# One transposing transfer per tile, side products one microsecond behind a freed PSUM bank, and weight loads ahead of turns on SP

## The chip, the cores and the metric

The kernel runs on one core of a Trainium2 chip. The metric is the device time of one execution in microseconds. Three runs of the kernel before gave 1275.52 to 1277.26 us, median 1276.15 us.

Engines are named as in the profile: PE does matmuls (PEld its weight loads), DVE element-wise work on vectors, ACT activation functions and copies, POOL the reductions over partitions, SP issues most DMA transfers.

## The reference, cut to what matters

Two layers, each a mixer of three branches (a retention, a gated linear recurrence "hgrn2", a differential attention) and a feed-forward block with a short convolution. There are 256 tokens behind 16 learned ones, so T = 272 columns; the model width is 1024 and everything is in 32-bit floats.

```python
for li in range(DEPTH):
    h = h + mixer(rms_norm(h, norm_mix_g[li]), w_in[li], w_branch[li], w_out[li], ...)
    h = h + conv_ffn(rms_norm(h, norm_ffn_g[li]), w_ffn_in[li], conv_w, conv_b, w_ffn_out[li], valid)
# mixer:
proj = hn @ w_in                      # 14 groups of columns: rq rk rv rg hq hf hi hg dq dk dv and three gates
branches = [retention(...), hgrn2(...), diff_attention(...)]
y = sum(sigmoid(gate_n) * (branch_n @ w_branch[n]))
return y @ w_out
```

Nearly all arithmetic is in the products with weights: `w_in`, three `w_branch`, `w_out`, `w_ffn_in` and `w_ffn_out`, all of which are streamed from memory once.

## The kernel before, in words

**Main products.** Activations lie with features on the partitions and the 272 tokens in the free direction. A weight tile is 128 by 128. To keep 32-bit precision with faster products, weights and activations are each cut into a high and a low part, and a tile takes three matmuls (lines 953 to 955): high by high, high weight by low activation, low weight by high activation. The last product of the second layer (`final`, lines 1593 to 1595) has weights as the moving side. The list `ORDER` names the products of a layer in their order: the columns of `w_in` (`hq`, `hf`, ..., `m2`), the branch products `b0`, `b1`, `b2`, then `wo`, `fi`, `fo`.

**Weights.** `_Weights.next` takes weights in chunks of eight tiles, 512 KB. For each chunk SP starts one transfer into `wraw` (three buffers), ACT copies it into `whi` with rounding (four buffers), DVE subtracts into `wlo` (four buffers). A chunk feeds 24 matmuls. The ACT and DVE instruction of a chunk carry `due`, the place in the plan's time at which the first matmul needs them; the transfer carries none.

**Side products.** The branches' own matmuls (recurrence levels `lev`, `px`, `pm`; outputs `ho` and `ro`; scores `s` and `ds`; attention outputs `do`) run on PE between main products. Their results lie in PSUM banks of two rotating buffers each, `bank` and `acc`. A bank is free again when the last instruction that reads it, on ACT or DVE, is done.

**Turns.** Where data has to be transposed, ACT copies the upper and the lower 16 bits of each 32-bit word into two planes (`apart`), SP starts a transposing transfer for each plane (`turned`), and ACT puts the planes together again. This happens in `to_tokens` (values of all branches, blocks of 128 columns, four to a plane), `flip` (one block to a plane), `da_rest` (three blocks to a plane) and `residual` (four). There are 61 such tiles, so 122 transposing transfers.

**The order of the work.** The program is first recorded as a list of operations, and a planner (`_Plan.order`) then simulates the engines with costs given in the code and emits all instructions in the order in which the simulation started them. On the chip each engine takes its instructions in this order and waits at each one for what it needs; an instruction that waits holds up all behind it on its engine. The names in the planner that matter here:

- `start(op, t)`: the earliest time at which an operation finds all buffers it needs (a buffer of a tag comes free when its last user is done, plus a lag).
- `rank(op, t)`: among operations of an engine that can start at the same time, the lowest rank goes first. A side product is not taken until the data that others gave it has been there for `SAFE` = 1.0 us. An operation whose `due` is less than `URGENT` = 3 ahead of the main product last started goes before everything else.
- `LAG`: time from the end of an operation until another engine may use its result; 2.0 us for SP's transfers.
- in `_Engine.call`: the cost of a transfer on SP is 0.06 us, plus its bytes over 360 GB/s, plus 0.7 us when it transposes. So a plane of four blocks counts 1.49 us, a weight chunk 1.52 us.
- `behind` and `settle` spread the side work of a branch over the main products that run beside it; `*b2` cuts the result of the differential attention into `b2hi` and `b2lo` for the product `b2`.

Of the kernel before, what the change touches and what calls it, by code (L numbers as in the profile page):

```python
# [21 lines left out]
P = 128  # L22
# [17 lines left out]
SLOTS = 13  # L40
# [8 lines left out]
HOLD, PULL = 3.0, 8.0  # L49
SAFE = 1.0  # L50
SURE = 0.3
URGENT = 3


BASE = {"rq": 0, "rk": 4, "rv": 8, "rg": 16, "hq": 24, "hf": 32, "hi": 40, "hg": 48,
# [300 lines left out]
class _Plan:  # L356
# [99 lines left out]
    def order(self):  # L456
# [29 lines left out]
        def start(op, t):  # L486

            want = {}
            for n in op.tiles:
                if n not in held:  # L490
                    want[self.tag[n]] = want.get(self.tag[n], 0) + 1
            for tag, k in want.items():
                if len(free[tag]) < k:
                    return None
                t = max(t, sorted(free[tag])[k - 1])
            return t

        def rank(op, t):
            if op.engine == "pe" and op not in mains:
                if op.fed + SAFE > t:  # L500
                    return math.inf
                return op.key - PULL if beside and op.fed + SURE <= t else op.key + HOLD
            if op.due - reached < URGENT:
                return op.due - 1000.0
            late = 8.0 if op.func in self.SETS and self.SETS[op.func] != tables else 0.0
            return op.key + late
# [4 lines left out]
        while len(out) < todo:  # L511
            best = None
            for e, t0 in engines.items():
                while later[e] and later[e][0][0] <= t0:
                    _, c, op = heapq.heappop(later[e])
                    now[e].append((c, op))
                found = None
                for c, op in now[e]:
                    t = start(op, t0)
                    if t is not None and (found is None or (t, rank(op, t), c) < found[:3]):  # L520
                        found = (t, rank(op, t), c, op)
                if later[e]:
                    t1 = later[e][0][0]
                    if found is None or t1 < found[0]:
                        found = (t1, 0.0, -1, None)
                if found is not None and (best is None or found[0] < best[0]):
                    best = found + (e,)
            if best is None:
                raise RuntimeError("no order: " + str([(e, [o.tiles for _, o in now[e]][:4]) for e in now]))
            t, _, c, op, e = best  # L530
            if op is None:
                engines[e] = t
                continue
            now[e].remove((c, op))
            cost = op.cost
            if op.func in self.SETS and self.SETS[op.func] != tables:
                tables = self.SETS[op.func]
                cost += self.SWITCH
                if tables == "le":
                    out.append(None)  # L540
                    todo += 1
            for n in op.tiles:
                if n not in held:
                    held.add(n)
                    f = free[self.tag[n]]
                    f.remove(min(f))
            if e == "pe":
                beside = op not in mains
                if not beside:
                    reached = op.key  # L550
            if e == "pool" and op.func is not None:
                if op.func != code:
                    code, t = op.func, max(t, engines[e] + self.RELOAD)
                engines["dve"] += self.SHARE * max(0.0, min(engines["dve"], t + cost) - t)
                sums.append((t, t + cost))
            if e == "dve":
                cost += self.SHARE * sum(max(0.0, min(b, t + cost) - max(a, t)) for a, b in sums[-2:])
            engines[e] = t + cost
            self.busy[e] += cost
            done = t + cost  # L560
            for n in op.tiles:
                left[n] -= 1
                if left[n] == 0:
                    free[self.tag[n]].append(done + self.LAG[e] + self.FREE)
            for o in op.after:
                o.need -= 1
                if o.engine != e:
                    o.fed = max(o.fed, done + self.LAG[e])
                o.ready = max(o.ready, done + (self.LAG if o.engine != e else self.SAME)[e])
                if o.need == 0:  # L570
                    push(o)
            for o in op.then:
                o.need -= 1
                o.ready = max(o.ready, done)
                if o.need == 0:
                    push(o)
            if op.run is not None:
                out.append(op)
            else:
                todo -= 1  # L580
# [12 lines left out]
class _Engine:  # L593
# [5 lines left out]
    def __getattr__(self, method):  # L599
        f = getattr(self.engine, method)  # L600

        def call(*args, **kw):
# [20 lines left out]
            if method == "reciprocal":  # L623
                cost += 7 * self.each * n
            elif method == "tensor_tensor_scan":
                cost += self.each * n
            elif method == "transpose":
                cost = 0.11
            elif method == "matmul":
                cost = max(0.218 if args[1].shape[-1] > 32 else 0.07, 4 * n / 2400 + 0.02)  # L630
            elif method == "dma_start":
                cost = self.fixed + self.each * n * outs[0].shape[0] + (0.7 if kw.get("transpose") else 0.0)
            self.plan.add(self.name, lambda: f(*args, **kw), cost, outs, ins, kind)  # L633

        return call
# [2 lines left out]
class _Weights:  # L638
# [13 lines left out]
    def next(self):  # L652
        c, i = divmod(self.used, CHUNK_TILES)
        self.used += 1
        if i == 0:
            due = self.plan.key
            room = [P, ROOM]
            raw = self.plan.tile(self.pool, [P, CHUNK_TILES * P], F32, "wraw", 3, f"wraw{c}")
            hi = self.plan.tile(self.pool, room, F32R, "whi", 4, f"whi{c}")
            lo = self.plan.tile(self.pool, room, F32R, "wlo", 4, f"wlo{c}")  # L660
            self.plan.key = due - LEAD
            pieces = 1 if c > 1 else 2
            for p in range(pieces):
                n = CHUNK_TILES // pieces
                cols = slice(p * n * P, (p + 1) * n * P)
                self.sp.dma_start(raw[:, cols], self.w[c][:, cols])
                order, places = self.places[c]
                mine = [[x[i] for i in order[p * n : (p + 1) * n]] for x in places]
                for first, outer, inner, dims in _boxes(*mine):
                    src = self.part(raw, (p * n + first) * P, inner * P, P, outer, inner)  # L670
                    to_hi, to_lo = (self.part(t, *x, outer, inner) for t, x in zip((hi, lo), dims))
                    self.act.activation(to_hi, src, AF.Copy)
                    self.dve.tensor_tensor(out=to_lo, in0=src, in1=to_hi.bitcast(F32), op=SUB)
                    for op in self.plan.ops[-2:]:
                        op.due = due
            self.plan.key = due
            self.cut = hi, lo
        return tuple(t[:, at[i] : at[i] + P] for t, at in zip(self.cut, self.places[c][1]))
# [16 lines left out]
def _trace(ctx, tc, plan, a, depth, probe):  # L695
# [298 lines left out]
    def planes(name, n):  # L994
        return new(tp, [P, 4 * T], U16, "vsrc", 4, name)[:, : 2 * n].rearrange("p (i x) -> p i x", i=2)

    def to_tokens(src, vt, e):

        apart, turned = planes("apart", 4 * P), planes("turned", 4 * P)
# [2 lines left out]
        for i in range(2):  # L1002
            act.activation(apart[:, i].rearrange("p (c f x) -> p c f x", c=2, f=2),
                           halves(src[:, :, : 2 * P], i).rearrange("p f (c x) -> p c f x", c=2), AF.Copy)
        for i in range(2):
            sync.dma_start(turned[:, i].rearrange("p (b x) -> p b x", x=P), apart[:, i], transpose=True)
        turned = turned.rearrange("p i (c x) -> p i c x", c=2)
        if top is None:
            for i in range(2):
# [10 lines left out]
    def flip(out, x):  # L1020
# [3 lines left out]
        halves = lambda t, i: t.bitcast(U16).rearrange("p (x two) -> p x two", two=2)[:, :, i]  # L1024
        for i in range(2):
            act.activation(apart[:, i], halves(x, i), AF.Copy)
        for i in range(2):
            sync.dma_start(turned[:, i].rearrange("p (b x) -> p b x", x=P), apart[:, i], transpose=True)
        for i in range(2):
            act.activation(halves(out, i), turned[:, i], AF.Copy)  # L1030

# [46 lines left out]
    for li in range(depth):  # L1078
# [365 lines left out]
        def da_rest(b, hd, sb, nm, sm, cf, tiles):  # L1444
# [17 lines left out]
            for i in range(2):  # L1462
                for c, n, at in ((0, 2 * P, P), (T, P, 0)):
                    act.activation(apart[:, i, at : at + n], halves(w[:, c : c + n], i), AF.Copy)
            for i in range(2):
                sync.dma_start(turned[:, i].rearrange("p (b x) -> p b x", x=P), apart[:, i], transpose=True)
            for i in range(2):
                act.activation(halves(a1[:, META : T + P], i), turned[:, i], AF.Copy)

# [73 lines left out]
        def residual():  # L1543
# [5 lines left out]
            for g, (t, c) in enumerate(((0, 0), (0, 1), (1, 0))):  # L1549
                apart, turned = planes("apart", 4 * P), planes("turned", 4 * P)  # L1550
                halves = lambda x, i: x.bitcast(U16).rearrange("p k (x two) -> p k x two", two=2)[:, :, :, i]
                for i in range(2):
                    act.activation(apart[:, i].rearrange("p (k x) -> p k x", k=4), halves(h[:, 4 * c : 4 * c + 4, META + t * P : META + (t + 1) * P], i), AF.Copy)
                for i in range(2):
                    sync.dma_start(turned[:, i].rearrange("p (b x) -> p b x", x=P), apart[:, i], transpose=True)
                for i in range(2):
                    act.activation(halves(st["old"][:, g : g + 1], i), turned[:, i].unsqueeze(1), AF.Copy)
                plan.key += 20.0
# [250 lines left out]
```

## Time and profile before

| what | value |
|---|---|
| median of three runs | 1276.15 us |
| lowest and highest | 1275.52, 1277.26 us |
| the profiled execution, its own time | 1276.58 us |
| its span, from the first to the last instruction | 1274.8 us |
| busy time of PE, PEld | 1261.6 and 1240.7 us |
| busy time of DVE, ACT, POOL | 964.8, 899.2, 115.5 us |
| granted clock of PE, mean | 0.999 |
| weight transfers on SP | 402 of 512 KB, 4 of 256 KB |
| transposing transfers on SP | 122 |
| DMA traffic | 230.49 MB, mean 181 GB/s |

How to read the rows: a row of the timeline has the start in us from the span's first instruction, the duration, the engine, the line, the operation, out<-in by the names in the code, and in brackets the idle time of that engine just before, with what ended it. Line 633 is the helper that records every operation, so rows of it are told apart by names. Matmuls overlap in the pipeline and their ends are modelled: a matmul with 272 columns shows some 0.28 us, but the next one starts 0.12 us after it. A short stop of PE is therefore best read from the distance of two starts, and PE's idle time shows less than the stop.

### The profile page before, as it was taken

The numbers are of one execution on the slowest core, as the hardware profiler recorded it, in microseconds if no ns is written. First come the engines' busy times: TensorE is split into PE (matmuls) and PEld (weight loads), VectorE is DVE, ScalarE is ACT, GpSimd is POOL, SyncE is SP. The second block draws the span as 40 slices with busy tenths as digits, with TensorE's granted clock in tenths as the row PEclk, the third lists the DMA queues.
The fourth block names the chain that finished last, engine by engine and source line by source line (L and its number), as shares of the span: only waits on it lengthen the run. The fifth ranks groups of instructions, "written<-read, shape, count | busy, mean of one in ns | idle before, by whom it ended". The sixth has DMA issues, their size and how long they took to land.

```text
span 1274.8 us, 28782 instructions
## 1 busy us (share of the span) xinstructions
PE 1261.6 (99%) x11612; PEld 1240.7 (97%) x11612; DVE 964.8 (76%) x1677; ACT 899.2 (71%) x1700; POOL 115.5 (9%) x89
## 2 busy tenths in 40 slices
PE   9999999999999999999999999999999999999998
PEld 9999999999999999999999999999999999999986
DVE  6797587899775789886576875878897868898854
ACT  6766687788797576665456567887788975787643
POOL 2000031101111000000010000411012210000000
PEclk9999999999999999999999999999999999999999
DMA  7655557556647546556555546475565566576663
GB/s 269 196 168 155 165 152 216 170 152 190 197 142 207 183 151 198 180 170 193 172 180 180 168 145 190 151 228 174 154 190 176 166 202 203 167 213 205 206 196 110
DMA packets 109205, 230.49 MB, mean 181 GB/s; under 512 B 55312, under 2 KB 55440, under 8 KB 109072
## 3 DMA queue, kind: packets, MB, share of 16 engines
q1 hardware_dynamic: 108784, 228.13, 58.0%
q8 instruction: 91, 1.49, 0.5%
q10 hardware_dynamic: 288, 0.52, 0.1%
q14 instruction: 42, 0.34, 0.1%
HBM read 216.16 MB, written 1.05 MB: 170 GB/s over the span
## 4 chain that ended last, share of the span: by engine, by line
PE 84%; issue 5%; DVE 3%; DMA 3%; ACT 3%; POOL 2%; SPq 0%; ACTq 0%; POOLq 0%; DVEq 0%
PE main L953 24%; PE main L955 24%; PE main L954 24%; DMA wraw<-in_w 3%; POOL hr L633 2%; PE fo L1593 2%; PE fo L1594 2%; PE fo L1595 2%; PE lev L1178 1%; DVE wlo L633 1%; PE fi L955 1%; PE fi L954 1%; PE fi L953 1%; ACT whi L633 1%; PE ds L1422 1%
## 5 line engine op out<-in xcount | busy, mean ns | idle before, releaser
L953 PE MATMUL main<-xh,whi 128*128 128x272 f32 (+1 forms) x2240 | 642.6, 287 | 0.7 <-ACT whi L633 0.7
L633 DVE TENSOR_TENSOR wlo<-wraw,whi 128x1024 fp32r<-128x1024 f32 (+1 forms) x411 | 498.4, 1217 | 188.6 <-ACT whi L633 183.1
L955 PE MATMUL main<-xh,wlo 128*128 128x272 f32 (+1 forms) x2240 | 636.9, 284 | 1.2 <-DVE wlo L633 1.0
L954 PE MATMUL main<-xl,whi 128*128 128x272 f32 (+1 forms) x2240 | 636.1, 284 | 1.0 <-issue 1.0
L633 ACT ACTIVATE whi<-wraw 128x1024 fp32r<-128x1024 f32 (+1 forms) x411 | 426.1, 1041 | 195.2 <-PE main L954 78.5
L955 PEld LDWEIGHTS main<-xh,wlo 128*128 128x128 f32 x2240 | 421.6, 188 | 3.5 <-DVE wlo L633 2.2
L953 PEld LDWEIGHTS main<-xh,whi 128*128 128x128 f32 x2240 | 421.7, 188 | 2.2 <-ACT whi L633 1.2
L954 PEld LDWEIGHTS main<-xl,whi 128*128 128x128 f32 x2240 | 421.7, 188 | 0.2
L633 POOL PARTITION_ALL_REDUCE hr<-hsq x36 | 76.9, 2155 | 426.6 <-ACT hsq L633 388.9
L633 DVE SCALAR_TENSOR_TENSOR two_b<-main,small,two_b 128x256 f32<-128x256 f32 (+2 forms) x128 | 54.6, 487 | 28.3 <-ACT two_b L633 28.2
L633 ACT ACTIVATE two_b<-main,small 128x272 f32<-128x272 f32 (+1 forms) x64 | 33.1, 566 | 28.1 <-PE main L955 28.1
L953 PE MATMUL main<-ghi,whi 128*128 128x272 f32 x176 | 50.8, 289 | 0.0
L954 PE MATMUL main<-glo,whi 128*128 128x272 f32 x176 | 50.6, 287 | 0.0
L955 PE MATMUL main<-ghi,wlo 128*128 128x272 f32 x176 | 50.3, 286 | 0.0
L955 PE MATMUL main<-b1hi,wlo 128*128 128x272 f32 (+1 forms) x128 | 36.6, 286 | 1.2 <-DVE wlo L633 1.2
L953 PE MATMUL main<-b0hi,whi 128*128 128x272 f32 (+1 forms) x128 | 37.3, 291 | 0.2 <-DVE y L633 0.2
L953 PE MATMUL main<-b1hi,whi 128*128 128x272 f32 (+1 forms) x128 | 37.1, 290 | 0.0
L953 PE MATMUL main<-yhi,whi 128*128 128x272 f32 (+1 forms) x128 | 36.4, 284 | 0.0
L955 PE MATMUL main<-yhi,wlo 128*128 128x272 f32 (+1 forms) x128 | 36.3, 284 | 0.0
L954 PE MATMUL main<-b0lo,whi 128*128 128x272 f32 (+1 forms) x128 | 36.3, 284 | 0.0
L954 PE MATMUL main<-b1lo,whi 128*128 128x272 f32 (+1 forms) x128 | 36.3, 284 | 0.0
L954 PE MATMUL main<-ylo,whi 128*128 128x272 f32 (+1 forms) x128 | 36.3, 284 | 0.0
(283 smaller groups left out, 2169.2 us busy)
## 6 DMA issues: line engine op xcount, KB each, us to landing
wraw<-in_w SPq DMA_DIRECT2D x402, 512.0 KB, 3.8
turned<-apart SPq DMA_TRANSPOSE x86, 2.7
h<-in_h SPq DMA_DIRECT2D x4, 272.0 KB, 5.6
dec<-in_dec SPq DMA_DIRECT2D x2, 544.0 KB, 6.1
wraw<-in_w SPq DMA_DIRECT2D x4, 256.0 KB, 5.2
const<-in_const SPq DMA_DIRECT2D x1, 937.0 KB, 5.4
turned<-turned SPq DMA_TRANSPOSE x36, 2.4
gain<-in_gl SPq DMA_DIRECT2D x1, 512.0 KB, 5.0
```

Source lines behind the costliest of these rows:

```text
L633: self.plan.add(self.name, lambda: f(*args, **kw), cost, outs, ins, kind)
L953: nc.tensor.matmul(o, wh, hi, start=first, stop=False)
L954: nc.tensor.matmul(o, wh, lo, start=False, stop=False)
L955: nc.tensor.matmul(o, wl, hi, start=False, stop=last)
L1178: nc.tensor.matmul(o, keys, x, start=True, stop=True)
L1422: nc.tensor.matmul(ss[m][:, at : at + nk], q[half, hd, q0 : q0 + P], k[half, hd, :nk], start=True, stop=True)
L1593: nc.tensor.matmul(o, gh, wh, start=first, stop=False)
L1594: nc.tensor.matmul(o, gl, wh, start=False, stop=False)
L1595: nc.tensor.matmul(o, gh, wl, start=False, stop=end)
```

## The change

The planner's rules change in three places, and the two transfers of a tile's planes become one.

```diff
-URGENT = 3
+URGENT = {"act": 4.5, "dve": 3.0, "sp": 12.0}
+TURN = "turn"
+STILL = 0.5
...
             for tag, k in want.items():
                 if len(free[tag]) < k:
                     return None
-                t = max(t, sorted(free[tag])[k - 1])
+                late = SAFE if op.engine == "pe" and op not in mains else 0.0
+                t = max(t, sorted(free[tag])[k - 1] + late)
             return t
...
-            if op.due - reached < URGENT:
+            if op.due - reached < URGENT.get(op.engine, 0.0):
                 return op.due - 1000.0
...
-                o.ready = max(o.ready, done + (self.LAG if o.engine != e else self.SAME)[e])
+                o.ready = max(o.ready, done + (self.LAG if o.engine != e else self.SAME)[e] + STILL * (o.func == TURN))
...
             elif method == "dma_start":
-                cost = self.fixed + self.each * n * outs[0].shape[0] + (0.7 if kw.get("transpose") else 0.0)
+                cost, kind = (1.3, TURN) if kw.get("transpose") else ( self.fixed + self.each * n * outs[0].shape[0], None)
...
                 self.sp.dma_start(raw[:, cols], self.w[c][:, cols])
+                fetch = self.plan.ops[-1]
...
                     for op in self.plan.ops[-2:]:
                         op.due = due
+                    fetch.due = due if c > SLOTS else math.inf
...
+    def turn(out, x):
+
+        sync.dma_start(out.rearrange("p i (b x) -> p (i b) x", x=P), x.rearrange("p i x -> p (i x)"), transpose=True)
+
...
-        for i in range(2):
-            sync.dma_start(turned[:, i].rearrange("p (b x) -> p b x", x=P), apart[:, i], transpose=True)
+        turn(turned, apart)
```

The last edit stands in `to_tokens`, `flip`, `da_rest` and `residual` alike. In words:

- **Banks.** A side product on PE, if it takes a new buffer, is planned no earlier than 1.0 us after that buffer came free. Main products keep the old rule.
- **Turns.** A tile's two planes go in one transfer, which the plan counts at 1.3 us whatever its size. `o.func == TURN` is asked of the operation that is to be made ready, so the 0.5 us of `STILL` lie between the ACT copies into the planes and the start of the transfer.
- **Weights.** From the 15th chunk on, the transfer of a chunk has a `due` too, and SP takes it before anything else that could start at the same time when its first matmul is less than 12 us of plan ahead. For ACT's copy into `whi` this distance grows from 3 to 4.5 us; for DVE it stays at 3. PE and POOL have no operations with a `due`.

More of the change, by code (lines that the diff above doesn't have):

```diff
@@ L1026, in flip @@
             act.activation(apart[:, i], halves(x, i), AF.Copy)
-        for i in range(2):
-            sync.dma_start(turned[:, i].rearrange("p (b x) -> p b x", x=P), apart[:, i], transpose=True)
+        turn(turned, apart)
         for i in range(2):
@@ L1464, in da_rest @@
                     act.activation(apart[:, i, at : at + n], halves(w[:, c : c + n], i), AF.Copy)
-            for i in range(2):
-                sync.dma_start(turned[:, i].rearrange("p (b x) -> p b x", x=P), apart[:, i], transpose=True)
+            turn(turned, apart)
             for i in range(2):
@@ L1553, in residual @@
                     act.activation(apart[:, i].rearrange("p (k x) -> p k x", k=4), halves(h[:, 4 * c : 4 * c + 4, META + t * P : META + (t + 1) * P], i), AF.Copy)
-                for i in range(2):
-                    sync.dma_start(turned[:, i].rearrange("p (b x) -> p b x", x=P), apart[:, i], transpose=True)
+                turn(turned, apart)
                 for i in range(2):
```

## The prediction

> **What bounds the kernel now.** I read the page first, then PE's busy time by stretches, then who PE waited for.
>
> ```profile
> span 1274.8 us, 28782 instructions
> PE 1261.6 (99%) x11612; PEld 1240.7 (97%) x11612; DVE 964.8 (76%) x1677; ACT 899.2 (71%) x1700; POOL 115.5 (9%) x89
> ```
> ```profile
> 0.00:23.00 23.00, 21.11 (x140) 19.82 (x141) 13.47 (x18) 15.15 (x24) 5.58 (x9) 1.00 0.79 255
> ...
> 200.00:400.00 200.00, 198.13 (x1596) 195.06 (x1595) 160.24 (x333) 165.44 (x393) 30.76 (x19) 1.00 0.63 180
> ...
> 900.00:1040.00 140.00, 137.54 (x1150) 134.49 (x1150) 111.19 (x247) 115.75 (x288) 23.70 (x14) 1.00 0.59 177
> ```
> ```profile
> PE main L955 <- DVE wlo L633: 2.2, 4, 0.8
> PE ro L1062 <- DVE ho L633: 1.1, 2, 0.8
> PE main L954 <- issue: 1.0, 1, 1.0
> ...
> PE main L953 <- ACT whi L633: 0.7, 2, 0.4
> PE do L633 <- DVE tw L633: 0.4, 1, 0.4
> ```
>
> PE sets the end: it is busy for 1261.6 of 1274.8 us at full clock (the 1.00 of each stretch), so no amount of faster side work counts unless PE stops for it. The stops lie where the branches run: 1.9 us of idle time in the first layer (200 to 400), 2.5 us in the second (900 to 1040). The list of waits names them: late weights, and `ro` products that wait for DVE's `ho`. The change adds and removes no matmul; it can only gain these stops, a few us out of 1276, and it can lose without such a limit, since the planner deals out the whole order anew. The start (first weights) and the 1.0 us that the profile puts down to nothing are out of its reach.
>
> **Part 1, the banks.** The regular distance of two main matmuls and the stops at side products:
>
> ```profile
> 30.14 0.29 PE L955 MATMUL main<-xh,wlo 128*128 128x272 f32 x1
> 30.26 0.28 PE L953 MATMUL main<-xh,whi 128*128 128x272 f32 x1
> ```
> ```profile
> 233.23 0.28 PE L633 MATMUL ro<-wts,rvt 128*128 128x144 f32 x1
> 233.83 0.39 PE L1062 MATMUL ro<-kt,rvt 128*128 128x272 f32 x1 [0.32 <-ACT tw L633]
> ```
> ```profile
> 242.97 0.36 PE L1062 MATMUL ro<-kt,rvt 128*128 128x272 f32 x1 [0.84 <-DVE ho L633]
> ```
> ```profile
> 242.38 0.79 DVE L633 TENSOR_TENSOR ho<-ro,hr 128x272 f32<-128x272 f32 x2 [1.07 <-ACT hr L633]
> ```
> ```profile
> 260.14 0.36 PE L1062 MATMUL ro<-kt,rvt 128*128 128x272 f32 x1 [0.25 <-DVE ho L633]
> ```
> ```profile
> 326.68 0.29 PE L955 MATMUL main<-b0hi,wlo 128*128 128x272 f32 x1
> 327.00 0.49 PE L633 MATMUL do<-tw,vs 128*128 128x128 f32 x2
> ```
>
> Two starts are 0.12 us apart (30.14 to 30.26). At 233.83 they are 0.60 apart: a stop of 0.48, of which the idle time shows 0.32, so the pipeline hides 0.16. With this 0.16 the stop at 242.97 is 1.00 and the one at 260.14 is 0.41. At 327.00 the distance is 0.32, a stop of 0.20. These four wait for the last reader of a bank: the two `ho` at 242.38 read the two `ro` banks of the head before, and `tw` reads the bank of `ret_tail`. Together 0.48 + 1.00 + 0.41 + 0.20 = 2.09 us.
>
> The edit puts such a product 1.0 us later in PE's order; main products fill the time. It removes no instruction. As the longest stop is just 1.00, it covers all four if the rest of the order stays as it is; I take 1.9 of the 2.09, since the last one is covered without any margin. Bounds: nothing (the readers come later by as much as the product), and 2.09. What it costs is delay of the branch, up to 1 us for each bank taken; that is free while the main products that need the branch are further away. That cover is thinnest before `b2` of the second layer:
>
> ```profile
> 1037.95 1.24 DVE L633 TENSOR_TENSOR b2lo<-da,b2hi 128x1032 fp32r<-128x1032 f32 x1 [0.35 <-ACT b2hi L633]
> ```
> ```profile
> 1039.88 0.28 PE L953 MATMUL main<-b2hi,whi 128*128 128x258 f32 x1
> ```
>
> The second half of `b2`'s input is done at 1039.19. `b2` starts at 1039.88 with four weight tiles for each of two outputs, 24 matmuls of 0.12, from the first half; the second half is needed at 1042.8. The slack is 3.6 us.
>
> **Part 2, one transfer for two planes.**
>
> ```profile
> L633 SPq DMA_TRANSPOSE turned<-apart x86: 1178/1234/2645, 120.1 to 1154.1; - x86
> ...
> L633 SPq DMA_TRANSPOSE turned<-turned x36: 1100/1176/1914, 131.8 to 1019.0; - x36
> ```
> ```profile
> turned<-apart SPq DMA_TRANSPOSE x86, 2.7
> ...
> turned<-turned SPq DMA_TRANSPOSE x36, 2.4
> ```
>
> A transfer of three or four blocks holds SP for 1.234 us, one of a single block for 1.176: three more blocks cost 0.06 us of issue and 0.3 us until landing. A joint transfer of eight blocks is not in the trace. Bounds: issue between 1.2 (as today's one) and 2.5 (as today's two); landing between 2.7 (as today's one) and 1.2 + 2.7 = 3.9 us (as today's second). By the small difference between one and four blocks I take the lower ends, 1.3 us of issue and 3.0 until landing. So 61 tiles give SP back 61 × 1.2 = 73 us in all, and a turn is complete about 0.9 us sooner. The joint transfer must wait for both copies of ACT, where the first plane used to go after its own copy; SP's second issue came 1.2 us after the first anyway, so this costs nothing while the copies are less than that apart. Behind a waiting turn on SP stand weight transfers; with one turn in place of two there is one such wait less per tile. None of this is on PE's path by itself, so I price it at nothing; it pays through part 3. The planned 1.3 us, with 0.5 ahead and the lag of 2.0 behind, leaves 0.3 us for landing beyond my 3.0.
>
> [...]
>
> **Part 3, weights ahead of turns.**
>
> ```profile
> 1011.12 3.54 SPq L633 DMA_DIRECT2D wraw<-in_w  x2
> 1014.81 1.19 SPq L633 DMA_TRANSPOSE turned<-apart  x1
> 1016.67 3.40 SPq L633 DMA_TRANSPOSE turned<-turned  x2
> 1020.12 1.25 SPq L633 DMA_TRANSPOSE turned<-apart  x1
> 1021.47 7.63 SPq L633 DMA_DIRECT2D wraw<-in_w  x4
> ```
> ```profile
> 1018.24 0.50 ACT L633 ACTIVATE hr<-hr,eps 128x242 f32<-128x242 f32 x1 [1.59 <-POOL hr L633]
> ...
> 1026.43 1.06 ACT L633 ACTIVATE whi<-wraw 128x1024 fp32r<-128x1024 f32 x1 [1.48 <-DMA wraw<-in_w]
> 1028.31 1.06 ACT L633 ACTIVATE whi<-wraw 128x1024 fp32r<-128x1024 f32 x1 [0.82 <-DMA wraw<-in_w]
> ```
> ```profile
> 1026.99 0.28 PE L955 MATMUL main<-xh,wlo 128*128 128x258 f32 x1
> 1027.54 0.39 PE L953 MATMUL main<-xh,whi 128*128 128x258 f32 x1 [0.27 <-ACT whi L633]
> 1027.77 0.28 PE L954 MATMUL main<-xl,whi 128*128 128x258 f32 x1
> 1028.80 0.39 PE L955 MATMUL main<-xh,wlo 128*128 128x258 f32 x1 [0.76 <-DVE wlo L633]
> ```
> ```profile
> 988.41 0.39 PE L955 MATMUL main<-b1hi,wlo 128*128 128x258 f32 x1 [0.76 <-DVE wlo L633]
> ```
> ```profile
> 379.66 0.39 PE L955 MATMUL main<-b1hi,wlo 128*128 128x272 f32 x1 [0.43 <-DVE wlo L633]
> ```
>
> Here the whole mechanism is in sight. ACT stands still for POOL until 1018.24; the second turn of the flip on SP waits behind that; from about 1014.7 (end of 3.54 us from 1011.12) to 1021.47 SP starts no weight. PE eats a chunk in 24 × 0.12 = 2.9 us, so more than two chunks are missing. When SP comes free they go out in a row; the first is copied at 1026.43, and PE stops at 1027.54 (0.55 between starts, a stop of 0.43) and at 1028.80 (1.03, a stop of 0.91). That is 1.34 us, and the edit aims at just this: a weight due within 12 us goes before a turn, the turn starts 0.5 us behind ACT's copies, and it is one issue instead of two. I take all 1.34. At 988.41 the idle time is the same 0.76, so the stop is again 0.91; no SP row is at fault there but the order on ACT and DVE. An `act` distance of 4.5 instead of 3 moves the copy 1.5 us up if the planner saw it as late; half of it, 0.45, I count as gained. At 379.66 (0.43 idle, 0.59 with the 0.16) DVE is late and its distance is unchanged: nothing. Part 3 gains 1.34 + 0.45 = 1.8, with bounds from 2.84 (all four) to nothing.
>
> What is moved back: a turn that lets a weight pass lands later. Two transfers in a row are copied at 1026.43 and 1028.31, so each weight in front costs some 1.9 us. On ACT, evacuations and exponentials stand behind an earlier `whi`, 1.06 us each; PE would notice only if a main bank came free late, and the list of waits has no such row now.
>
> **The sum.** A new order brings new stops by chance; data that comes late (0.4 behind `tw` in the list, more such in other places) is in no edit's reach. I put 0.3 us for them, between nothing and the 2.8 of late weights that this order has. So −1.9 − 1.8 + 0.3 = −3.4 us. The profiled execution took 1276.58 us, 1.78 more than its span; it becomes 1273.2. It lies 0.43 above the median of the three runs, so the median becomes 1272.75.
>
> **The rivals.**
>
> *New stops for old ones.* Stops of 0.4 to 1.0 us are errors of the planner's costs, which the edits do not mend except at the banks; late weights turn up elsewhere, because ACT still waits for POOL and SP still takes its order. For it: three of the late weights have three different causes (SP, ACT, DVE). Against it: one of them is what the edit addresses. Then only part 1 stays: 1276.15 − 1.9 = 1274.3.
>
> *Everything goes.* Both groups vanish, 2.09 + 2.84, with no new ones: 1276.15 − 4.9 = 1271.2, perhaps some tenths less where fewer side products part the main ones.
>
> *The differential attention of the second layer comes late* (the one on the other side). Place: `b2` of layer two with 3.6 us of slack. On the way there in the last pair of heads are two `wts` turns and the flip of the tails, and four products that take banks. Each bank costs up to 1.0 us; each weight that passes a turn 1.9; each turn gains 0.9. With one weight per turn this is 4 + 5.7 − 2.7 = 7.0 us late, 3.4 over the slack, which only eats the gain of 3.4: no change. It ends slower from 3.6 + 3.4 + 2.6 = 9.6 us on. With two weights per turn it is 12.7 late, PE stops for 9.1, and the time is 1276.15 − 3.4 + 9.1 = 1281.9. For it: 12 us of `due` reach over four chunks. Against it: `wraw` has three buffers, so two weights can rarely go in front of the same turn, and the first layer's branches have more room.
>
> *The joint transfer is as slow as two*, so that SP is held as long as before and the change does not do what it says: parts 1 and the ACT half of 3 remain, 1276.15 − 1.9 − 0.45 = 1273.8.
>
> **How the numbers follow.** I count a difference under 0.2% (2.6 us) as none, which is about what a measurement of this kernel can tell from no change. Forecast 1272.75 with its neighbours below 1273.6: 0.40. Everything goes, 1271.2: 0.12. New stops for old ones, 1274.3, with the attention late by one weight per turn: 0.24. Joint transfer slow, 1273.8: 0.06. Attention late by more, or another branch so, around 1279 to 1282: 0.18. So faster 0.52, the same 0.30, slower 0.18. The range from 1270.4 to 1279.5 leaves out some 0.06 below and 0.12 above. The forecast's own range, by the bounds of parts 1 and 3, is 1271.2 to 1273.6.
>
> **What would show it.** Part 1 is right if no `ro` or `do` row among PE's waits has a reader of a bank behind it. Part 2: 61 transposing transfers, about 1.3 us of issue, landing near 3.0. Part 3: no stretch of 7 us without a weight on SP around the second layer's flips, and less than 1 us for PE behind `whi` and `wlo` between 200 and 1040. The forecast falls if PE waits for `b2hi` or `b2lo`, or if its stops between 200 and 1040 add up to the same 4.4 us as now.

## The result, and the profile after

| | before | after |
|---|---|---|
| median of 19 runs each, us | 1275.62 | 1278.31 |
| lowest to highest, us | 1272.37 to 1277.59 | 1276.70 to 1282.40 |
| ratio, 95% interval | | 1.0024 (1.0016 to 1.0031) |
| profiled execution: own time, span, us | 1276.58, 1274.8 | 1278.09, 1276.3 |

The changed kernel is slower by a quarter of a per cent, where 3.4 us less had been forecast. That is a small loss, but the interval leaves out both no change and any gain. The page of the kernel after shows the same work:

```profile
span 1276.3 us, 28715 instructions
PE 1261.5 (99%) x11612; PEld 1240.7 (97%) x11612; DVE 968.5 (76%) x1677; ACT 896.3 (70%) x1700; POOL 115.0 (9%) x89
```

PE is as busy as before to 0.1 us, so only its stops differ. Its list of waits (engine, output and line, what ended the wait; total us, times, longest):

```profile
PE do L636 <- DVE tw L636: 1.5, 1, 1.5
PE main L958 <- issue: 1.2, 1, 1.2
...
PE do L1069 <- DVE dm L636: 0.9, 2, 0.7
PE main L958 <- DVE two_b L636: 0.8, 1, 0.8
PE ro L1069 <- DVE ho L636: 0.7, 1, 0.7
...
PE do L1069 <- DVE da L636: 0.6, 1, 0.6
PE main L960 <- DVE wlo L636: 0.4, 2, 0.2
PE do L1070 <- DVE near L636: 0.4, 1, 0.4
```

In the two stretches where the branches run PE is idle for 1.57 and 2.85 us, 4.4 us together and as much as before; the prediction had named that as a sign that it falls:

```profile
200.00:400.00 200.00, 198.43 (x1601) 195.64 (x1600) 161.13 (x331) 162.06 (x385) 27.83 (x17) 1.00 0.66 182
...
900.00:1040.00 140.00, 137.15 (x1152) 134.43 (x1151) 115.04 (x247) 115.88 (x290) 21.20 (x14) 1.00 0.64 182
```

Late weights (`wlo`) fell from 2.2 to 0.4 us, as part 3 promised. In their place stand side products: `tw` and `near` are made from turned data, and `dm`, `ho` and `da` are the last readers of banks. So PE now waits for branches (the side work of retention, recurrence and attention) that are late. What they wait for is seen one engine further, in the view of the tile `turned`: SP's transfers (issue time in ns, smallest, median, largest), then how long ACT stood idle in front of a copy out of a turn until its transfer had landed (us, times), then the time to landing (us). First the kernel after:

```profile
L636 SPq DMA_TRANSPOSE turned<-apart x43: 1210/1232/2412, 120.0 to 1155.8; - x43
...
L636 SPq DMA_TRANSPOSE turned<-turned x18: 1167/1171/2369, 129.3 to 1021.1; - x18
...
  DMA turned<-apart: 13.5, 14
  DMA turned<-turned: 4.2, 2
...
  ACT old L636: 1.8, 2
...
DMA to landing us min/median/max: 2.3/3.7/6.2
```

(`old` is the share of the residual's copies in those waits) and the same lines of the kernel before:

```profile
  DMA turned<-apart: 7.8, 7
  DMA turned<-turned: 6.1, 5
...
  ACT old L633: 0.4, 1
...
DMA to landing us min/median/max: 2.2/2.5/6.2
```

The joint transfer's issue is what was taken for it (1.232 us for six or eight blocks, 1.171 for two). Its landing is not: the median is 3.7 us, and 3.9 for the larger ones (`turned<-apart`), where the plan allows 1.3 + 2.0 = 3.3. In this profile 38 of the 61 land later than that.

Which of them land late can be read from the same trace. I counted, for each turn of six or eight blocks, how many weight transfers (for two turns one of them is the load of `dec`, 544 KB) were issued ahead of it on SP and had not landed when it went out. In the kernel after, 5 turns had none in front of them and landed after 2.8 us in the median, 21 had one (3.2 us) and 17 had two (4.9 us).

The longest stop, at `do<-tw`, can be followed back through four engines. SP:

```profile
1017.35 3.62 SPq L636 DMA_DIRECT2D wraw<-in_w  x3
1021.06 2.37 SPq L636 DMA_TRANSPOSE turned<-turned  x1
```
ACT, then DVE, then PE:
```profile
1024.60 1.06 ACT L636 ACTIVATE whi<-wraw 128x1024 fp32r<-128x1024 f32 x1 [2.24 <-DMA wraw<-in_w]
...
1027.20 0.34 ACT L636 ACTIVATE tails<-turned 128x128 uint16<-128x128 uint16 x1
```
```profile
1025.70 2.57 DVE L636 TENSOR_TENSOR wlo<-wraw,whi 128x1024 fp32r<-128x1024 f32 x2 [2.03 <-ACT whi L636]
...
1028.56 0.76 DVE L636 TENSOR_TENSOR tw<-tails,const 128x128 f32<-128x128 f32 x1
```
```profile
1027.65 0.28 PE L960 MATMUL main<-xh,wlo 128*128 128x258 f32 x1
1029.47 0.46 PE L636 MATMUL do<-tw,vs 128*128 128x128 f32 x2 [1.54 <-DVE tw L636]
```

The turn goes out behind three weights, its issue alone takes 2.37 us, and it lands 5.0 us after its start, at 1026.1. The first copy out of it runs at 1027.20, 6.1 us after that start, since ACT had stood 2.24 us for a weight of the same queue and was busy with the next one when the turn landed. DVE, which makes `wlo` of both weights, takes `tw` only after that, and PE, whose order has `do` in front of the next main products, stands for 1.7 us (1.82 between starts, less the usual 0.12). So this stop has two late inputs, a turn and a weight, and this profile alone does not part them.

### The profile page after: what moved, and what is told of

Read it like the earlier page. It is cut to its first block, busy times and chain, and to the rows that moved or that the text cites. A ratio compares the mean times of both kernels' runs of the same rounds, so it can differ in the third digit from the quotient of the medians.

```text
span 1276.3 us, 28715 instructions
## 1 busy us (share of the span) xinstructions
PE 1261.5 (99%) x11612; PEld 1240.7 (97%) x11612; DVE 968.5 (76%) x1677; ACT 896.3 (70%) x1700; POOL 115.0 (9%) x89
## 3 DMA queue, kind: packets, MB, share of 16 engines
q8 instruction: 91, 1.49, 0.5%
## 4 chain that ended last, share of the span: by engine, by line
PE 66%; issue 10%; ACT 8%; DVE 8%; DMA 6%; POOL 2%; SPq 0%; ACTq 0%; DVEq 0%; POOLq 0%
PE main L958 19%; PE main L959 19%; PE main L960 19%; DMA wraw<-in_w 3%; ACT whi L636 3%; DVE wlo L636 3%; DMA turned<-apart 2%; POOL hr L636 2%; PE fo L1600 2%; PE fo L1598 2%; PE fo L1599 2%; ACT apart L636 1%; PE lev L1185 1%; DVE two_b L636 1%; PE fi L959 1%
## 5 line engine op out<-in xcount | busy, mean ns | idle before, releaser
L960 PE MATMUL main<-b0hi,wlo 128*128 128x272 f32 (+1 forms) x128 | 36.3, 284 | 0.0
```

Of the source, the lines that this page charges most:

```text
L960: nc.tensor.matmul(o, wl, hi, start=False, stop=last)
```

## The experiments

The theory: with 1.3 us for a turn the plan sets its users about 1 us too early, so ACT, and behind it PE, wait in their fixed order. The rivals: the joint transfer is slow on the chip whatever the order; the bank rule delays the branches; any new order loses. All ratios are to the kernel before, timed beside each kernel (its medians there were 1275.1 to 1275.8 us), with 95% intervals. The columns behind the ratio come from one profiled execution each. "Stops" adds up, from the trace of each profiled execution, how far the start of a PE matmul lies behind the usual distance for its shape, wherever that is over 0.13 us (without the first 23 us and the regular gaps inside `lev`, `ds` and `pm`). "ACT at turns" is the sum of the two idle rows shown above.

| kernel | median us | ratio | span | stops | ACT at turns |
|---|---|---|---|---|---|
| before | 1275.6 | 1 | 1274.8 | 7.8 | 13.9 |
| after | 1278.3 | 1.0024 (1.0016 to 1.0031) | 1276.3 | 9.3 | 17.7 |
| before's order, joint transfer | 1279.3 | 1.0032 (1.0020 to 1.0043) | 1275.7 | 9.3 | 30.9 |
| the same, two transfers in the residual | 1275.3 | 0.9998 (0.9989 to 1.0007) | 1272.4 | 5.5 | 24.2 |
| after's order, two transfers | 1283.8 | 1.0064 (1.0045 to 1.0083) | 1282.3 | 13.5 | 15.0 |
| turn rule alone | 1282.4 | 1.0050 (1.0036 to 1.0064) | 1285.4 | 14.8 | 21.9 |
| bank rule alone | 1276.6 | 1.0005 (0.9994 to 1.0016) | 1273.7 | 6.3 | 8.9 |
| weight rule alone | 1272.3 | 0.9977 (0.9966 to 0.9988) | 1268.4 | 2.8 | 8.2 |
| weight rule, ACT's part alone | 1274.6 | 1.0000 (0.9990 to 1.0010) | 1275.5 | 8.0 | 13.8 |
| bank and weight rule | 1281.2 | 1.0048 (1.0032 to 1.0063) | 1278.6 | 11.3 | 7.5 |
| after, turn's users 0.5 us later | 1273.3 | 0.9980 (0.9969 to 0.9991) | 1271.6 | 6.0 | 7.9 |
| after, 1.0 us later | 1272.4 | 0.9974 (0.9966 to 0.9983) | 1271.5 | 4.6 | 2.4 |
| after, 2.0 us later | 1272.2 | 0.9974 (0.9963 to 0.9985) | 1270.6 | 4.5 | 0.3 |
| after, 1.0 later in the residual alone | 1278.7 | 1.0033 (1.0019 to 1.0046) | 1279.5 | 10.0 | 17.7 |
| after, 1.0 later in all the rest | 1272.5 | 0.9981 (0.9972 to 0.9990) | 1270.8 | 4.3 | 4.2 |
| after without the bank rule | 1281.1 | 1.0044 (1.0027 to 1.0061) | 1279.4 | 10.0 | 17.2 |
| the same, 1.0 us later | 1273.3 | 0.9979 (0.9969 to 0.9989) | 1272.4 | 6.0 | 2.4 |
| before, dealt anew | 1274.8 | 0.9996 (0.9987 to 1.0006) | 1273.0 | 6.7 | 11.5 |

Span less stops lies between 1265.6 and 1270.6 us in every row while the spans differ by 17: so the stops are most of what tells these kernels apart.

**Which part loses?** The chip's share was taken first, with every order but SP's held fixed: the first transfer of a pair is left out, the second moves both planes (and goes out earlier where a copy would otherwise read too soon).

```diff
 # before, in _Plan.issue, for each pair (a, b) of planned transfers
+            order.remove(a)
+            place = min([order.index(b)] + [order.index(o) for o in a.after if o in order])
...
+        whole = (out.rearrange("p i (b x) -> p (i b) x", x=P), x.rearrange("p i x -> p (i x)"))
...
+        b = plan.add("sp", lambda: nc.sync.dma_start(*whole, transpose=True), cost, [out[:, 1]], [x[:, 1]], "second")
```

> Before's order on PE, DVE, ACT and POOL, unchanged; only the first of each pair of turning transfers is left out and the second moves both planes. Theory (the new order gives a turn too little time, the transfer itself is no worse): that order left 1.49 + 1.49 + 2.0 us for a pair of four blocks, the joint transfer lands sooner than the second one did, so the time is that of before or up to 2 us less (ratio 0.998 to 1.000). Rival (the joint transfer is slow on the chip, or holds SP or the weights up): 1277 us or more, ratio over 1.001.

It came out with the rival, 1.0032. PE's waits of that kernel name a place, copies in the second layer's feed-forward (`two_b`), and show a longer wait at `do`:

```profile
PE main L967 <- DVE wlo L645: 2.1, 4, 1.1
PE do L645 <- DVE tw L645: 2.1, 1, 2.1
...
PE main L965 <- ACT two_b L645: 1.3, 2, 0.8
```

The other way round, after's orders with two transfers at the place of one:

```diff
-        sync.dma_start(out.rearrange("p i (b x) -> p (i b) x", x=P), x.rearrange("p i x -> p (i x)"), transpose=True)
+        def run():
+            for i in range(2):
+                nc.sync.dma_start(out[:, i].rearrange("p (b x) -> p b x", x=P), x[:, i], transpose=True)
+        plan.add("sp", run, 1.3, [out], [x], TURN)
```

> After's order on PE, DVE, ACT and POOL, unchanged; at the place of each joint transfer the two old ones go out one behind the other. Theory (turns come too late for the new order): the second plane lands about 1 us later still, so more stops, 1 to 4 us above after: ratio to before 1.003 to 1.006. Rival (the new order is bad for reasons that have nothing to do with turns): as after, 1.0024 within 0.0007.

1.0064, a little above what the theory had given: the new order does mind when a turn lands. The residual's share of the first of these two was told apart by leaving the old loop in its three tiles:

```diff
 # before's order; to_tokens, flip and da_rest as in the first experiment, residual:
+                for i in range(2):
+                    sync.dma_start(turned[:, i].rearrange("p (b x) -> p b x", x=P), apart[:, i], transpose=True)
-                turn(turned, apart)
```

> As the first experiment (before's order on PE, DVE, ACT and POOL unchanged, joint transfers), but the three tiles of the residual keep their two transfers. Theory A (the loss of that experiment is made where the copies of the two planes stand far apart in ACT's order and now both wait for the later transfer, in the second layer's feed-forward): the time comes back to before, 1275 to 1277 us, ratio 0.9995 to 1.001. Theory B (joint transfers lose everywhere): ratio 1.0025 to 1.0035, about 1279 us.

The loss is gone (0.9998). In the profiles, 2.9 us of stops between 1120 and 1164 us go with it; another 1.5 us less at `do` (1022 us) lie ahead of the residual, in a part that both kernels order alike, and so show how much single executions differ. In before's order the copies out of the residual's two planes stand up to 5 us apart on ACT:

```profile
1115.56 0.79 ACT L633 ACTIVATE old<-turned 128x512 uint16<-128x512 uint16 x1
...
1120.57 0.79 ACT L633 ACTIVATE old<-turned 128x512 uint16<-128x512 uint16 x1
```

There the joint transfer came too late for that order. ACT waits even more for turns than in the kernel after, 24.2 us, without harm:

```profile
  DMA turned<-apart: 18.0, 15
  DMA turned<-turned: 6.2, 3
```

So these waits of ACT by themselves are no loss (0.9998); I take it that one becomes a loss where what is behind it is due, and that before's order has room for that: it allowed 1.49 + 1.49 + 2.0 = 4.98 us for a tile of two planes of four blocks. (1.49 is what the plan's code gives for such a plane; it counts four bytes for each two-byte element.)

**The rules one by one.** The bank rule, the turn rule and the weight rule were each put into the kernel before. The bank rule:

```diff
-                t = max(t, sorted(free[tag])[k - 1])
+                late = SAFE if op.engine == "pe" and op not in mains else 0.0
+                t = max(t, sorted(free[tag])[k - 1] + late)
```

> Before with the bank rule alone. Theory (late turns): turns are planned as before, so the bank rule may show its gain, 1273.5 to 1275.6 us, ratio 0.998 to 1.000. Rival (the bank rule delays the branches): 1277 to 1279 us, ratio 1.001 to 1.003. If any new order costs something, a ratio near 1.001 to 1.002 with new stops at unlike places.

1.0005: neither gain nor loss shown, and the interval leaves out the 1.9 us of part 1. The waits for `ho` are gone from the list, but in the second layer `b2` now waits for the attention:

```profile
PE main L954 <- ACT b2hi L634: 1.5, 1, 1.5
...
PE main L955 <- DVE b2lo L634: 1.1, 2, 0.9
```

The turn rule, as after less the other two:

```diff
 # against after
-                late = SAFE if op.engine == "pe" and op not in mains else 0.0
+                late = 0.0
-URGENT = {"act": 4.5, "dve": 3.0, "sp": 12.0}
+URGENT = {"act": 3.0, "dve": 3.0}
```

> Before with the joint transfer, its planned 1.3 us and the 0.5 us ahead of it alone; bank rule and weight rule as before. Theory (late turns): all of the loss is here, 1278 to 1280 us, ratio 1.002 to 1.0035, with the products behind turns and the copies out of turns among the waits. Rival (bank rule): no loss, 1274 to 1276 us.

1.0050, all of the loss and more.

The weight rule:

```diff
 # against before
-URGENT = 3
+URGENT = {"act": 4.5, "dve": 3.0, "sp": 12.0}
-            if op.due - reached < URGENT:
+            if op.due - reached < URGENT.get(op.engine, 0.0):
+                fetch = self.plan.ops[-1]
+                    fetch.due = due if c > SLOTS else math.inf
```

> Before with the weight rule alone (due for SP's transfers at 12 us, 4.5 us for ACT's copies). Theory (late turns): part of the loss, as weights go in front of the two old transfers, 1276 to 1278 us. Rival (the rule gains what it aims at): 1273.5 to 1275 us, waits of main products for whi and wlo between 200 and 1040 under 1 us.

0.9977: the rival was right, and the rule gains. The size is 1.5 to 4.3 us by the interval, which holds the 1.8 of the forecast. ACT's half alone, with no `due` for SP:

```diff
 # against before
-URGENT = 3
+URGENT = {"act": 4.5, "dve": 3.0}
...
-            if op.due - reached < URGENT:
+            if op.due - reached < URGENT.get(op.engine, 0.0):
```

> Before with nothing but ACT's distance for the copies into whi at 4.5 instead of 3 us; SP's transfers carry no due. If the gain of the weight rule is ACT's: 1272 to 1273.5 us, ratio 0.997 to 0.998. If it is SP's, which was the larger part in the forecast: 1275 to 1276 us.

1.0000: no gain of ACT's half is shown (the interval, 1.3 us to either side, would hide its 0.45). The gain needs SP's `due`; that alone was not tried. Bank rule and weight rule together, the two edits above in one kernel:

> Before with the bank rule and the weight rule, turns in two transfers and planned as before. Theory (the two rules are sound and the turn alone loses): 1271 to 1273.5 us, ratio 0.996 to 0.998, as far down as the weight rule alone or a little further. Rival (they do not add up, or the new order loses by itself): 1274 us or more.

Here the theory failed: 1.0048. The gains do not add up, and the profile shows why in one row:

```profile
PE main L956 <- ACT b2hi L634: 6.8, 1, 6.8
```

`b2` of the second layer starts at 1032.4 us on the half of its input that is there; at 1038.6 PE comes to the other half and stands for 6.8 us until `b2hi` is done. That is the rival of the forecast in which the attention comes late, in the place that it named, but made by the bank rule and the weight rule with the old turns (the bank rule alone gave the two waits above, the weight rule alone none). In the kernel after, whose plan has one turn of 1.3 us, `b2hi` is done at 1035.4 us and no such row exists.

**Is it the turn's time in the plan?** The decisive test adds a delay for the users of a turn and changes nothing else in the planner's rules:

```diff
-... + STILL * (o.func == TURN))
+... + STILL * (o.func == TURN) + 1.0 * (op.func == TURN))
```

> After, with whatever uses a turn planned 1.0 us later (4.3 us from the start of the transfer instead of 3.3). Theory (turns come too late for the plan): the loss goes, 1273.5 to 1276 us, ratio 0.998 to 1.0005, fewer waits behind turned tiles. Rival (the joint transfer hurts others, or any new order does): stays at 1277 to 1280 us.

0.9974, a larger gain than the theory had expected. The view of `turned`:

```profile
  DMA turned<-apart: 2.4, 2
...
DMA to landing us min/median/max: 2.3/3.7/7.0
```

The transfers land no sooner than in the kernel after, yet ACT waits 2.4 us instead of 17.7, and PE's list holds no reader of a bank any more:

```profile
PE do L636 <- DVE tw L636: 1.0, 1, 1.0
PE main L960 <- issue: 1.0, 1, 1.0
...
PE main L958 <- ACT whi L636: 0.4, 1, 0.4
PE main L960 <- DVE wlo L636: 0.4, 2, 0.2
PE main L959 <- issue: 0.3, 1, 0.3
```

As any new order might be lucky, the dose was varied (0.5 and 2.0 in place of 1.0), and a control dealt before's order anew by a hair:

```diff
 # against after, for 0.5; for 2.0 the same with 2.0
-... + STILL * (o.func == TURN))
+... + STILL * (o.func == TURN) + 0.5 * (op.func == TURN))
 # control, against before
-    LAG = {"pe": 0.20, "act": 0.13, "dve": 0.12, "pool": 0.15, "sp": 2.0}
+    LAG = {"pe": 0.20, "act": 0.13, "dve": 0.12, "pool": 0.15, "sp": 2.05}
```

> After, with the users of a turn planned 0.5 us later. Theory: in between, 1273.5 to 1277 us, some waits behind turned tiles left. Rival (luck): anywhere, 1277 us or more as likely.

> After, with the users of a turn planned 2.0 us later. Theory (the plan lacks about 1 us per turn): the loss stays away, 1271 to 1274 us, unless the attention of the second layer then comes late for b2, seen as a wait for b2hi. Rival (the good result at 1.0 was a lucky order): 1275 us or more without such a wait.

> A control: before with one cost of the plan changed by a hair, the lag of SP's transfers 2.05 us instead of 2.0. No rule is changed, but a like share of the order is dealt anew. If a new order alone costs something: ratio over 1.001. If the order before is nothing special: 1274.5 to 1277 us, ratio 0.999 to 1.001.

With 0, 0.5, 1.0 and 2.0 us the medians are 1278.3, 1273.3, 1272.4 and 1272.2, and ACT's idle time at turns is 17.7, 7.9, 2.4 and 0.3. Half a microsecond already gives most of it back, a little more than the theory had put in between. The control's time does not differ from before's (0.9996); it is a weak one, as it puts another instruction in 328 of the 1605 places of ACT's order, where the delay of 1.0 us does so in 751. Luck is not ruled out for any single row, but all five kernels of the table in which the values' and the attention's turns have the longer time gain, by 1.9 to 3.3 us, and all four orders planned with 3.3 us for these turns (after, turn rule alone, after without the bank rule, later in the residual alone) lose.

**Where?** The profile after had suggested the residual, where its copies wait 1.8 us. The delay was put there alone, which moves 11 rows of ACT's order and 7 of DVE's, and then everywhere else:

```diff
 # against after; "last" marks the residual's turns; the second kernel has 1.0 and 0.0 the other way round
+MORE = {"turn": 0.0, "last": 1.0}
-... + STILL * (o.func == TURN))
+... + STILL * (o.func in MORE) + (MORE[op.func] if op.func in MORE else 0.0))
```

> After, with the users of a turn planned 1.0 us later in the three tiles of the residual alone; PE's, POOL's and SP's orders stay as they are, 11 rows of ACT's and 7 of DVE's change place. Theory (copies out of turns that land late hold up ACT, and with it the evacuation of main banks): of the 4.3 us or so between after and the kernel with all turns planned later, about 2 come back, 1275.5 to 1277 us, ratio 1.000 to 1.001, and PE no longer waits for two_b near 1142. Rival (the loss is in the attention's and the values' turns): stays at 1278 us.

> After, with the users of a turn planned 1.0 us later everywhere but in the residual. Theory: the other half, 1273.5 to 1276 us, ratio 0.998 to 1.000. If the residual is the only place: 1278 us.

1.0033 and 0.9981: the residual is not the place, and the reading of the single profile was wrong. The loss lies with the other turns, those of the values and of the attention, whose delay alone brings back as much as the delay of every turn, as far as the runs can tell (0.9981 and 0.9974).

**The bank rule beside the turn.** After without it, and the same with a turn's users 1.0 us later:

```diff
 # against after, and against after with 1.0 us more
-                late = SAFE if op.engine == "pe" and op not in mains else 0.0
+                late = 0.0
```

> After without the bank rule. Theory (the turn's plan loses, the bank rule with it gains up to 2 us): 1278 to 1281 us, with waits of side products for readers of banks. Rival (the bank rule is what loses, as it did with the old turns and the weight rule, where b2 waited 6.8 us): 1272 to 1276 us.

> After without the bank rule and with the users of a turn planned 1.0 us later. Theory: the turn is mended, so only the bank rule's share is missing, 1272.5 to 1275 us, some waits for readers of banks. Rival (the bank rule loses): 1270 to 1272 us.

Without the bank rule the kernel after is slower by the medians, 1.0044 against 1.0024, but the intervals overlap; with the turns mended it makes no difference that the runs can tell, 0.9979 against 0.9974. So the rule may pay where branches are late; where they are not, no gain of it is shown.

## Why the prediction was wrong

**The step that failed** is in part 2: "I take the lower ends, 1.3 us of issue and 3.0 until landing", "None of this is on PE's path by itself, so I price it at nothing", with the remark that the plan leaves "0.3 us for landing beyond my 3.0". The issue was right. The landing came to 3.7 us in the median, near the bound of 3.9 that the text had and set aside; the 0.3 us of room were gone in 38 of 61 turns. The price was not nothing: 1278.3 − 1272.4 = 5.9 us between the same kernel without and with 1 us more in the plan. The 3.0 was not a bad guess at the transfer itself: in before's order the joint transfer landed after 3.1 us in the median. The order made from the cheaper plan is what moved it, by the count above: in before's order 4 of the 43 turns of six or eight blocks went out with two weights in front of them (median 4.9 us) and 39 with one or none (3.1 us), in the new order 17 did. I looked at the transfer and did not follow the plan's new number to those who rely on it: ACT's copies and PE's side products were moved ahead by the 1.7 us between 4.98 and 3.3 (1.2 if counted from ACT's copies, as the plan keeps 0.5 in front of the transfer). The turn was not "complete about 0.9 us sooner": for the larger tiles the time from the first issue until both planes had landed was 3.8 us in the median before and 3.9 after.

**Part 1** (−1.9): what it says was not seen in the kernel after, where `ho`, `dm` and `da` still stop side products for 2.2 us, as I read it because the readers themselves are late by more than the margin. It is seen where turns have their time: with 1.0 us more, no such row is left, and without the bank rule 0.5 us of them (`ho` 0.3, `da` 0.2), far from 1.9. By itself the rule moved the stop to `b2` of the second layer.

**Part 3** (−1.8): the effect came, with late `wlo` down to 0.4 us. For the rule alone its size agrees with the runs (1.5 to 4.3 us); ACT's 0.45 is neither shown nor ruled out. In the kernel after, the weight rule has little left to do: with the turn rule it gives 1.0044 where the turn rule alone gives 1.0050, intervals that overlap widely, and without SP's `due` the plan of the kernel after would differ in 6 of SP's 480 places. I take it that the joint transfer had already freed SP, so that parts 2 and 3 share a gain; a kernel with the longer turns and without the weight rule, which would show it, was not run.

**The sum** of −3.4 is right for the mended kernel (1272.4 against 1272.75); that this is due to the single terms is not shown, since part 1 came out far smaller than stated, and the agreement may be luck.

**The rivals.** The attention that comes late has its place right and its size nearly (8 us of stops at `b2` with bank and weight rule, where it gave 9.1), but the kernel after has none of it: `b2` does not wait. "The joint transfer is as slow as two" is refuted for SP's time: six or eight blocks issue in 1.232 us in the median, as three or four did (1.234 in the kernel before). "New stops for old ones" comes nearest: stops of 0.4 to 1.7 us at other places, though by a cause that can be named. The range held the time; the direction was wrong.

## What to carry to other kernels

Where a fixed order comes from a plan, a cheaper operation is two changes: what it costs on its engine, and when its users are set to start. Price the second by the slowest half of the landings among other traffic, not by a quiet one (here 4.9 us in the median behind two weights, 2.8 with none in front), and leave the users the room that they had. Effects of rules need not add up: the weight rule gains alone (0.9977), the bank rule alone changes nothing that shows (1.0005), and both together lose (1.0048). So run them together, and look at the input that comes last for each product (here `b2`).

## What the runs showed of the hardware

- A transposing transfer's issue on SP hardly grows with its size in the range seen: in the median 1.18 us for one block, 1.17 for two, 1.23 for three or four and for six or eight. Single issues took up to 2.6 us in the kernel before and 2.4 in the kernel after.
- Its landing does depend on order. The larger joint transfers took 3.1 us in the median in before's order and 3.9 in after's, at least 2.7 and at most 6.2 us there. They went with the weights in front: with two of these not yet landed the median was 4.9 us in either order, with one 3.1 and 3.2, with none 3.1 and 2.8. This is a count from two traces; moving the weights alone was not tried.
- Executions of one kernel differ by 5 us (1272.4 to 1277.6 for the kernel before), more than the change is worth. A single profile pointed at the wrong place once here.
